# A float32 hybrid decoder layer on one core: Strassen products in the feed-forward matmuls, with the SwiGLU output kept in DRAM

## The chip, the cores and the metric

The kernel runs on one core of one Trainium2 chip. The metric is the device time of one execution in microseconds (us), lower is better. A core has engines that run side by side, each in its own order of instructions: TensorE (PE; its weight loads are listed apart as PEld), VectorE (DVE), ScalarE (ACT), GpSimd (POOL) and SyncE (SP), which here issues the DMA transfers of the weights. An engine waits for another one through semaphores.

## The reference, cut to what matters

One decoder layer for a sequence of 256 rows and a width of 2048, all in float32: a norm, an input projection, four token-mixer branches, their gated sum, an output projection, and then the feed-forward part, which is what the change touches (`w_ffn_gate` and `w_ffn_up` are 2048x5632, `w_ffn_down` is 5632x2048).

```python
        h = h + mixed @ w_out[l]
        v = rms_norm(h, norm_ffn[l])
        h = h + (jax.nn.silu(v @ w_ffn_gate[l]) * (v @ w_ffn_up[l])) @ w_ffn_down[l]
    return rms_norm(h, norm_final)
```

## The kernel before, in words

**Numbers in two parts.** A float32 factor is split into a high part (float32r, `whi`, `vth`, `hth`) and the rest (`wlo`, `vtl`, `htl`). A product of two such factors is three matmuls: high times high, high times low, low times high (`mm3`, L123 to L127). One matmul takes a 128x128 block of the activations, held transposed, as its weights and 512 columns of a weight matrix as the moving tile, and adds into a PSUM bank of 128x512.

**Weights.** `wpiece` (L112 to L121) loads 256 rows x 512 columns (512 KB, `raw`, five buffers) with a DMA issued by SP. ACT makes the high part of it (`whi`) and DVE the low part (`wlo`), each in one instruction of 128x1024. These 256 rows are called a K pair here: two blocks of 128 of the dimension summed over.

**A chunk.** `chunk` (L134 to L153) computes 512 output columns for both halves of the 256 rows, into two accumulators `acc`; of those there are four banks by turns, so that a chunk can begin while the last one is read. After the second K pair of a chunk it runs what waits in the list `later`, which is the transposing (`to_T`, L163) of the result before, on PE, ACT and DVE.

**Order of the work around the change.** Phase 3 (L645 to L671) has four chunks with `w_out`; from their result `hn` come `vth` and `vtl`, 16 blocks of K. Phase 4 (L673 to L686) has 11 steps `f`; each is one chunk with the gate matrix, SiLU on ACT, one chunk with the up matrix, and a product on DVE (`hd`); its transposed parts `hth` and `htl` stay on the core. Phase 5 (L688 on) has four chunks with `w_ffn_down` over 44 blocks of K, adds them to `hn`, and norms and stores the result. A tile framework lays each engine's instructions in order and puts a wait on a buffer where it is used again; the memory of a closed pool is given to later pools (`mx.close()`, L666, frees `mth` and `mtl`, the activations of phase 3), and then the first use of the new tile waits for the last use of the old one.

## Time and profile before

| | before |
|---|---|
| device time of three runs | 1540.54, 1544.31, 1544.32 us, median 1544.31 |
| profiled execution: span from first to last instruction | 1539.9 us |
| PE busy in the span | 1525.9 us (99%) |
| weight loads of PE | 1261.3 us (82%) |
| DVE busy | 837.8 us (54%) |
| ACT busy | 706.7 us (46%) |
| DMA | 292.11 MB, mean 190 GB/s |

The profiled execution is shown by its span; a time of its own beside it is not given. The span lies 0.6 us below the fastest of the three runs and 4.4 us below their median. Busy shares say how much of the span an engine worked, and not what it was waited for.

### The profile page before, as it was taken

To read this page: it belongs to the slowest core of one execution; us is meant where nothing else is said; L and a number is where in the kernel's file an instruction comes from. 1 tells how busy PE (TensorE), PEld (TensorE's weight loads), DVE (VectorE), ACT (ScalarE), POOL (GpSimd) and SP (SyncE) were. 2 spreads that over 40 slices of the span, in tenths; PEclk is the share of its full clock that TensorE was granted. 3 is DMA by queue.
4 is the path that set the end of the run, shared out by engine and by line. 5 is a ranking of instruction groups with operands and counts; after the bars stand their busy time and mean duration, and the time that the engine had idled before them with its cause. 6 is when DMAs were issued, how large, how long until landed. Compare 5 with 4: busy or idle time off the path is not lost.

```text
span 1539.9 us, 18236 instructions
## 1 busy us (share of the span) xinstructions
PE 1525.9 (99%) x6949; PEld 1261.3 (82%) x6949; DVE 837.8 (54%) x963; ACT 706.7 (46%) x864; POOL 94.8 (6%) x97
## 2 busy tenths in 40 slices
PE   9999999999999999999999999999999999999997
PEld 7878888888888888888888888888888888888886
DVE  5756645775565555555555455544445555444453
ACT  6545744544444444444544444444444444344342
POOL 3000300011111021010000000000000000000000
PEclk9999999999999999999999999999999999999999
DMA  8755555566666676767566666666666666666663
GB/s 256 221 150 152 158 170 152 174 182 204 200 203 198 199 206 197 205 194 243 179 182 189 190 189 188 192 186 195 188 188 191 191 190 215 193 191 193 193 193 107
DMA packets 150247, 292.11 MB, mean 190 GB/s; under 512 B 9552, under 2 KB 11664, under 8 KB 150032
## 3 DMA queue, kind: packets, MB, share of 16 engines
q1 hardware_dynamic: 148160, 285.28, 61.6%
q0 software_dynamic: 1968, 5.67, 1.4%
q8 instruction: 54, 0.88, 0.2%
q14 instruction: 33, 0.27, 0.0%
q10 hardware_dynamic: 32, 0.01, 0.0%
HBM read 288.82 MB, written 2.10 MB: 189 GB/s over the span
## 4 chain that ended last, share of the span: by engine, by line
PE 98%; DVE 1%; issue 0%; DMA 0%; POOL 0%; ACT 0%; SPq 0%; POOLq 0%; ACTq 0%
PE acc L127 94%; PE ps L159 2%; DMA xq<-in_x_dram 0%; PE ps L382 0%; PE ps L578 0%; PE ps L401 0%; PE ps L340 0%; DVE wlo L59 0%; PE ps L448 0%; PE ps L595 0%; PE ps L534 0%; PE ps L520 0%; PE ps L518 0%; POOL rq_y L59 0%; POOLq L745 0%
## 5 line engine op out<-in xcount | busy, mean ns | idle before, releaser
L59 DVE TENSOR_TENSOR wlo<-raw,whi 128x1024 fp32r<-128x1024 f32 (+1 forms) x536 | 665.6, 1242 | 654.2 <-ACT whi L56 653.2
L56 ACT ACTIVATE whi<-raw 128x1024 fp32r<-128x1024 f32 (+1 forms) x536 | 564.7, 1054 | 752.5 <-PE acc L127 709.7
L127 PE MATMUL acc<-wlo,uth 128*128 128x512 f32 (+1 forms) x832 | 323.6, 390 | 0.0
L127 PE MATMUL acc<-whi,utl 128*128 128x512 f32 (+1 forms) x832 | 323.1, 389 | 0.0
L127 PE MATMUL acc<-whi,uth 128*128 128x512 f32 (+1 forms) x832 | 317.8, 390 | 0.6 <-DVE nat L63 0.4
L127 PE MATMUL acc<-whi,vth 128*128 128x512 f32 x704 | 274.9, 390 | 0.0
L127 PE MATMUL acc<-whi,vtl 128*128 128x512 f32 x704 | 274.0, 389 | 0.0
L127 PE MATMUL acc<-wlo,vth 128*128 128x512 f32 x704 | 273.9, 389 | 0.0
L127 PEld LDWEIGHTS acc<-wlo,uth 128*128 128x128 f32 x832 | 156.9, 189 | 31.7 <-issue 1.0
L127 PEld LDWEIGHTS acc<-whi,utl 128*128 128x128 f32 x832 | 156.9, 189 | 31.4 <-issue 0.7
L127 PEld LDWEIGHTS acc<-whi,uth 128*128 128x128 f32 x832 | 154.2, 188 | 31.7 <-issue 0.7
L127 PEld LDWEIGHTS acc<-whi,vtl 128*128 128x128 f32 x704 | 132.2, 188 | 27.5
L127 PEld LDWEIGHTS acc<-whi,vth 128*128 128x128 f32 x704 | 132.2, 188 | 27.1
L127 PEld LDWEIGHTS acc<-wlo,vth 128*128 128x128 f32 x704 | 132.2, 188 | 27.0
L127 PE MATMUL acc<-whi,hth 128*128 128x512 f32 x352 | 137.0, 389 | 0.0
L127 PE MATMUL acc<-whi,htl 128*128 128x512 f32 x352 | 136.9, 389 | 0.0
L127 PE MATMUL acc<-wlo,hth 128*128 128x512 f32 x352 | 136.9, 389 | 0.0
L127 PEld LDWEIGHTS acc<-wlo,hth 128*128 128x128 f32 x352 | 66.1, 188 | 13.8
L127 PEld LDWEIGHTS acc<-whi,hth 128*128 128x128 f32 x352 | 66.1, 188 | 13.7
L127 PEld LDWEIGHTS acc<-whi,htl 128*128 128x128 f32 x352 | 66.1, 188 | 13.6
L127 PE MATMUL acc<-whi,mth 128*128 128x512 f32 x128 | 50.8, 397 | 0.0
L127 PE MATMUL acc<-wlo,mth 128*128 128x512 f32 x128 | 50.5, 395 | 0.0
...
## 6 DMA issues: line engine op xcount, KB each, us to landing
raw<-in_w_in_dram SPq DMA_DIRECT2D x192, 512.0 KB, 4.2
raw<-in_w_ffn_gate_dram SPq DMA_DIRECT2D x88, 512.0 KB, 4.4
raw<-in_w_ffn_up_dram SPq DMA_DIRECT2D x88, 512.0 KB, 3.8
raw<-in_w_ffn_down_dram SPq DMA_DIRECT2D x88, 512.0 KB, 4.8
raw<-in_w_branch_dram SPq DMA_DIRECT2D x32, 512.0 KB, 4.2
raw<-in_w_out_dram SPq DMA_DIRECT2D x32, 512.0 KB, 4.7
...
bb<-in_b_gate_dram POOLq DMA_DIRECT2D x16, 256.0 KB, 4.4
```

The costliest lines, as they stand in the source:

```text
L56: return nc.scalar.activation(o, i, f, **kw)
L59: return (eng or nc.vector).tensor_tensor(out=o, in0=a, in1=b, op=op)
L127: m = nc.tensor.matmul(acc, x_, w_, start=st, stop=sp_)
L159: nc.tensor.transpose(pt[:, i * S + t * P:i * S + (t + 1) * P], nat[:, t, (c0 + i) * P:(c0 + i + 1) * P], ident)
```

## The change

**Strassen pairs.** Of two gate and up (or two down) columns blocks of 512, and of a K pair, the old kernel makes eight block products (two row halves, two K blocks, two column blocks). Now some K pairs are made in seven products, in Winograd's form of Strassen's method: `s_weights` loads both weight blocks (`sx`, two DMAs of 512 KB), makes sums of them on DVE (`se`, and in place in `sx`), splits the four tiles in `sx` into `sh` and `sl` (128x2048) and the three in `se` into `seh` and `sel` (128x1536). The sums on the activation side are made by `s_sums` and kept in `vsh` and `vsl`. In each gate/up step the pairs are `FS` = 0, 3 and 5 of eight (0 and 3 in the first step), in each half of the down projection `DS` = 0, 3, 6, 9 and 12 of 22.

**`pair` in place of `chunk`.** It does two column blocks at once, in all eight PSUM banks, each in one buffer (`p1` to `p8`). Four hold the result of the plain products (`p2`, `p3`, `p4`, `p8`), four the Strassen products that have to be combined (`p1`, `p5`, `p6`, `p7`). After the last Strassen pair `mid` combines these on ACT and DVE (`mid_sums`, tiles `u`), and then runs the list `later`; the transposing uses the banks of `p1`, `p5`, `p6` and `p7`.

**SwiGLU output through DRAM.** `hid_out` transposes `hd` and writes it as float32 to DRAM by a DMA on POOL's queue. The down projection reads it back per K pair (`hv`, 256 KB, on SP) in each of its two halves, splits it anew into `ah`, and makes the sums for its Strassen pairs. `hv` lies in the tags `u1` and `u3` by turns, which are also the tags of two tiles of `mid_sums`; each has one buffer.

**Others.** `raw` has four buffers in place of five; the scratch pool `fp` has one buffer for each tag in place of two; all sums of the four blocks of `mid` go to `hn` in the down projection.

```diff
-        raw = wp.tile([P, nk, n], F32, tag="raw", name="raw", bufs=5)
+        raw = wp.tile([P, nk, n], F32, tag="raw", name="raw", bufs=4)
...
+                if also is not None and (kt0 + i) // 2 in also[0]:
+                    s_i = also[0].index((kt0 + i) // 2)
+                    v = late["tmp"].tile([P, 512], F32, tag="u1", name="sv").rearrange("p (a b) -> p a b", a=2)
+                    for j in range(2):
+                        act(v[:, j, :], pt[:, j * S:(j + 1) * S], scale=gcol(i + j))
+                    s_sums(v, also[1][:, s_i], also[2][:, s_i])
...
+    def s_sums(v, sh, sl):
+        w = late["tmp"].tile([P, 512], F32, tag="u0", name="ssum").rearrange("p (a b) -> p a b", a=4)
+        a11, a21, a12, a22 = v[:, 0, 0:P], v[:, 0, P:S], v[:, 1, 0:P], v[:, 1, P:S]
+        tt(w[:, 0, :], a21, a22, ALU.subtract)
+        tt(w[:, 1, :], w[:, 0, :], a11, ALU.subtract)
+        tt(w[:, 2, :], a11, a21, ALU.subtract)
+        tt(w[:, 3, :], a12, w[:, 1, :], ALU.add)
+        act(sh, w)
+        tt(sl, w, rd(sh), ALU.subtract)
+    def mm3s(acc, a, w, first, last, pin=False):
+        for x_, w_, st, sp_ in ((a[0], w[0], first, False), (a[0], w[1], False, False), (a[1], w[0], False, last)):
+            m = nc.tensor.matmul(acc, x_, w_, start=st, stop=sp_)
+            if pin:
+                tc.keep_in_program_order(m)
...
+    def s_weights(wl, wr, kp, sx):
+        rows = slice(kp * 2 * P, (kp + 1) * 2 * P)
+        x_ = sx.tile([P, 4, 512], F32, tag="sx", name="sx", bufs=2)
+        nc.sync.dma_start(x_[:, 0:2, :], wr[rows, :].rearrange("(k p) n -> p k n", p=P))
+        nc.sync.dma_start(x_[:, 2:4, :], wl[rows, :].rearrange("(k p) n -> p k n", p=P))
+        e = sx.tile([P, 3, 512], F32, tag="se", name="se", bufs=1)
+        h, lo = (sx.tile([P, 4, 512], F32R, tag=t, name=t, bufs=2) for t in ("sh", "sl"))
+        eh, el = (sx.tile([P, 3, 512], F32R, tag=t, name=t, bufs=2) for t in ("seh", "sel"))
+        tt(e[:, 0, :], x_[:, 0, :], x_[:, 1, :], ALU.add)
+        tt(x_[:, 0, :], x_[:, 0, :], x_[:, 2, :], ALU.add)
+        tt(e[:, 1, :], x_[:, 0, :], x_[:, 1, :], ALU.add)
+        tt(e[:, 2, :], e[:, 1, :], x_[:, 3, :], ALU.add)
+        act(h, x_)
+        tt(lo, x_, rd(h), ALU.subtract)
+        act(eh, e)
+        tt(el, e, rd(eh), ALU.subtract)
+        t1, r2, l1, l2 = ((h[:, i, :], lo[:, i, :]) for i in range(4))
+        t3, t2, t4 = ((eh[:, i, :], el[:, i, :]) for i in range(3))
+        return l1, l2, r2, t1, t2, t3, t4
+    def pair(wl, wr, nkp, skps, a_of, sx, mid, split=0):
+        pq = late["psum"]
+        names = (1, 5, 7, 6, 2, 3, 4, 8) if skps else (2, 3, 4, 8)
+        b = {i: pq.tile([P, 512], F32, tag=f"p{i}", name=f"p{i}") for i in names}
+        left = {2: nkp * 2 - len(skps), 3: nkp * 2 - len(skps), 4: nkp * 2 - len(skps), 8: 2 * (nkp - len(skps))}
+        for i in (1, 5, 6, 7):
+            left[i] = len(skps)
+        begun = set()
+        def go(i, a, w, pin=False):
+            left[i] -= 1
+            mm3s(b[i], a, w, i not in begun, left[i] == 0, pin)
+            begun.add(i)
+        held = []
+        for kp in range(nkp):
+            blk, sums = a_of(kp, kp in skps)
+            if kp in skps:
+                l1, l2, r2, t1, t2, t3, t4 = s_weights(wl, wr, kp, sx)
+                go(1, blk(0, 0), l1)
+                go(5, sums(0), t1)
+                go(7, sums(2), t3)
+                go(6, sums(1), t2)
+                go(2, blk(1, 0), l2)
+                go(3, sums(3), r2)
+                go(4, blk(1, 1), t4)
+                if kp == skps[-1]:
+                    mid(b)
+                continue
+            if not skps and kp == 2:
+                mid(b)
+            rows = slice(kp * 2 * P, (kp + 1) * 2 * P)
+            lh, ll = wpiece(wl[rows, :], 2, 512)
+            rh, rl = wpiece(wr[rows, :], 2, 512)
+            todo = [(i, [(blk(j, t), (wh[:, j, :], wl_[:, j, :])) for j in range(2)])
+                    for i, t, wh, wl_ in ((2, 0, lh, ll), (3, 0, rh, rl), (4, 1, lh, ll), (8, 1, rh, rl))]
+            if kp >= nkp - split:
+                held.append(todo)
+                continue
+            for i, prods in todo:
+                for a, w in prods:
+                    go(i, a, w)
+        for q in range(4):
+            for todo in held:
+                i, prods = todo[q]
+                for a, w in prods:
+                    go(i, a, w, pin=True)
+        return b
...
+    FS = (0, 3, 5)
+    late["tmp"] = fp
+    vsh = fp.tile([P, len(FS), 4, P], F32R, name="vsh")
+    vsl = fp.tile([P, len(FS), 4, P], F32R, name="vsl")
...
+    ps_early.close()
+    late["psum"] = ctx.enter_context(tc.tile_pool(name="pq", bufs=1, space=bass.MemoryType.PSUM))
+    sx = ctx.enter_context(tc.tile_pool(name="sxp", bufs=1))
...
+    def hid_out(hd, f):
+        hs = fp.tile([P, 4, S], F32, tag="hs", name="hs")
+        for i in (0, 2):
+            pt = trans_bank(hd, i, 2)
+            act(hs[:, i:i + 2, :].rearrange("p a b -> p (a b)"), pt)
+        d = dr.tile([P, 4, S], F32, name=f"hid{f}")
+        nc.gpsimd.dma_start(d, hs)
+        hid.append(d)
...
+    def mid_sums(b):
+        u = [fp.tile([P, 512], F32, tag=f"u{i}", name="u") for i in range(4)]
+        act(u[0], b[1])
+        tt(u[2], u[0], b[6], ALU.add)
+        tt(u[1], u[2], b[7], ALU.add)
+        tt(u[2], b[5], u[2], ALU.subtract)
+        tt(u[3], b[5], u[1], ALU.subtract)
+        return u
...
     for f in range(DFF // 512):
         fs = slice(f * 512, (f + 1) * 512)
-        ag = chunk(w_fg[:, fs], vth, vtl, NKT)
+        kept = []
+        def mid(b):
+            kept.extend(mid_sums(b))
+            run_later()
...
         hd = fp.tile([P, 2, 512], F32, tag="hd", name="hd")
         for t in range(2):
-            act(hd[:, t, :], ag[t], AF.Silu, scale=rstd2[:, t:t + 1])
-        au = chunk(w_fu[:, fs], vth, vtl, NKT)
-        for t in range(2):
-            stt(hd[:, t, :], au[t], rstd2[:, t:t + 1], hd[:, t, :], ALU.mult, ALU.mult)
-        later.append(lambda hd=hd, f=f: to_T(hd, hth, htl, 4 * f))
-    # ================= phase 5: down projection, final norm =================
+            tt(hd[:, t, :], kept[t], b[(2, 4)[t]], ALU.add)
+            act(hd[:, t, :], hd[:, t, :], AF.Silu, scale=rstd2[:, t:t + 1])
+            tt(kept[2 + t], kept[2 + t], b[(3, 8)[t]], ALU.add)
+            stt(hd[:, t, :], kept[2 + t], rstd2[:, t:t + 1], hd[:, t, :], ALU.mult, ALU.mult)
+        later.append(lambda hd=hd, f=f: hid_out(hd, f))
...
+    ah = uv.tile([P, 4, 2, 2 * S], F32R, tag="tl", name="ah")
+    DS = (0, 3, 6, 9, 12)
+    def h_of(kp, with_sums):
+        v = fp.tile([P, 512], F32, tag=("u1", "u3")[kp % 2], name="hv").rearrange("p (a b) -> p a b", a=2)
+        nc.sync.dma_start(v, hid[kp // 2][:, kp % 2 * 2:kp % 2 * 2 + 2, :])
+        q = kp % 4
+        act(ah[:, q, 0, :], v.rearrange("p a b -> p (a b)"))
+        tt(ah[:, q, 1, :], v.rearrange("p a b -> p (a b)"), rd(ah[:, q, 0, :]), ALU.subtract)
+        if with_sums:
+            i = DS.index(kp) % len(FS)
+            s_sums(v, hsh[:, i], hsl[:, i])
+        def blk(j, t):
+            o = slice(j * S + t * P, j * S + (t + 1) * P)
+            return ah[:, q, 0, o], ah[:, q, 1, o]
+        return blk, lambda n: (hsh[:, i, n, :], hsl[:, i, n, :])
...
+    for cc in range(2):
+        cols = [slice((2 * cc + i) * 512, (2 * cc + i + 1) * 512) for i in range(2)]
+        def mid(b):
+            u = mid_sums(b)
+            for t in range(2):
+                for i in range(2):
+                    o = hn[:, t, cols[i]]
+                    tt(o, o, u[2 * i + t], ALU.add)
+            run_later()
+        b = pair(w_fd[:, cols[0]], w_fd[:, cols[1]], NFT // 2, DS, h_of, sx, mid, split=2 if cc else 1)
```

In the excerpts that follow, each row is an instruction: line, operation, out<-in, size, and in brackets the engine or DMA queue whose semaphore it waits for. Line numbers are those of the kernel that the row is from. A name ends in a number that tells one buffer's use from another.

**First place: SP, from the last weights of the output projection on, before.**

```order
L114 DMA raw_6353<-in_w_out_dram 128x2x512 [waits DMAHW6_49,DVE_49]
L114 DMA raw_6371<-in_w_out_dram 128x2x512 [waits DMAHW7_49,DVE_49]
L114 DMA raw_6416<-in_w_ffn_gate_dram 128x2x512 [waits DMAHW0_49,DVE_49]
L114 DMA raw_6434<-in_w_ffn_gate_dram 128x2x512 [waits DMAHW1_49,DVE_49]
L114 DMA raw_6470<-in_w_ffn_gate_dram 128x2x512 [waits DMAHW2_49,DVE_49]
```

The same place on SP after the change.

```order
L120 DMA raw_6538<-in_w_ffn_up_dram 128x2x512 [waits DMAHW4_49,DVE_49]
L120 DMA raw_6632<-in_w_ffn_gate_dram 128x2x512 [waits DMAHW5_49,DVE_49]
L120 DMA raw_6638<-in_w_ffn_up_dram 128x2x512 [waits DMAHW6_49,DVE_49]
L120 DMA raw_6668<-in_w_ffn_gate_dram 128x2x512 [waits DMAHW7_49,DVE_49]
L220 DMA sx_6459<-in_w_ffn_up_dram 128x2x512 [waits DMASW3_49,DMASW4_49,DMASW2_49,DMASW5_49,DMASW1_49,DMASW6_49,DMASW0_49,DMASW7_49,PE_49,Pool_49]
L221 DMA sx_6459<-in_w_ffn_gate_dram 128x2x512
L220 DMA sx_6568<-in_w_ffn_up_dram 128x2x512
L221 DMA sx_6568<-in_w_ffn_gate_dram 128x2x512
L120 DMA raw_6674<-in_w_ffn_up_dram 128x2x512 [waits DMAHW0_49,DVE_49]
```

Behind the last load of `w_out` stand seven `raw` loads now, the last four of which are shown (K pairs 2 and 4, and the gate half of 5), and only then the loads of `sx_6459`, for K pair 0; the first of the two waits for PE and POOL: the pool of `sx` takes memory of `mth` and `mtl`, and its first tile waits for the last matmul that reads them.

**Second place: DVE, from the last gate/up step to the down projection, before** (`acc_9691` and `acc_9692` are that step's up chunk, `raw_9895` is a tile of `w_ffn_down`).

```order
L59 TENSOR_TENSOR wlo_9898<-raw_9895,whi_9897 128x1024 [waits DMAHW7_49,Activation_49]
L67 SCALAR_TENSOR_TENSOR hd_9688<-acc_9691,rstd2_6397,hd_9688 128x512 [waits PE_49]
L67 SCALAR_TENSOR_TENSOR hd_9688<-acc_9692,rstd2_6397,hd_9688 128x512 [waits PE_49]
L59 TENSOR_TENSOR wlo_9916<-raw_9913,whi_9915 128x1024 [waits DMAHW0_49,Activation_49]
L59 TENSOR_TENSOR wlo_9934<-raw_9931,whi_9933 128x1024 [waits DMAHW1_49,Activation_49]
```

The same place on DVE after the change (`hv_10118` is K pair 0 of the down projection, `hv_10166` K pair 1).

```order
L60 TENSOR_TENSOR hd_10096<-u_10001,p4_9779 128x512 [waits PE_49]
L60 TENSOR_TENSOR se_10388<-sx_10385 128x512 [waits DVE_49]
L60 TENSOR_TENSOR wlo_10213<-raw_10210,whi_10212 128x1024 [waits DMAHW5_49,Activation_49]
L60 TENSOR_TENSOR u_10003<-u_10003,p8_9780 128x512 [waits PE_49]
L68 SCALAR_TENSOR_TENSOR hd_10096<-u_10002,rstd2_6429,hd_10096 128x512 [waits DVE_49,Activation_49]
L60 TENSOR_TENSOR se_10388<-se_10388,sx_10385 128x512 [waits DVE_49]
L60 TENSOR_TENSOR wlo_10219<-raw_10216,whi_10218 128x1024 [waits DMAHW6_49,Activation_49]
L68 SCALAR_TENSOR_TENSOR hd_10096<-u_10003,rstd2_6429,hd_10096 128x512 [waits DVE_49,Activation_49]
L60 TENSOR_TENSOR ssum_10122<-hv_10118 128x128 [waits DMAHW3_49]
L60 TENSOR_TENSOR ssum_10122<-hv_10118 128x128
L60 TENSOR_TENSOR ssum_10122<-ssum_10122,hv_10118 128x128 [waits DVE_49]
L60 TENSOR_TENSOR ah_10109<-hv_10118,ah_10109 128x512 [waits Activation_49]
```

And SP there, after the change (before, only loads of `raw` stood there).

```order
L120 DMA raw_10298<-in_w_ffn_down_dram 128x2x512 [waits DMAHW1_49,DVE_49]
L120 DMA raw_10304<-in_w_ffn_down_dram 128x2x512 [waits DMAHW2_49,DVE_49]
L852 DMA hv_10118<-hid0_7034 128x512 [waits DMAHW3_49,DMASW1_49,DVE_49]
L120 DMA raw_10338<-in_w_ffn_down_dram 128x2x512 [waits DMAHW5_49,DMAHW4_49,DVE_49]
L120 DMA raw_10344<-in_w_ffn_down_dram 128x2x512 [waits DMAHW6_49,DVE_49]
L852 DMA hv_10166<-hid0_7034 128x512 [waits DVE_49]
L852 DMA hv_10206<-hid1_7366 128x512 [waits DMAHW3_49,DMASW2_49,DMAHW7_49,DVE_49,Activation_49]
L852 DMA hv_10246<-hid1_7366 128x512 [waits DMAHW6_49,DMAHW0_49,DVE_49]
```

The step's own results are now joined from six sums with `u` tiles and two products, with sums and splits for K pairs of the down projection between them. The load of `hv_10118` uses the tag `u1` and stands behind the reading of `u_10001`; that of `hv_10166` uses `u3` and stands behind the reading of `u_10003` (`hd_10096<-u_10003`).

**Third place: DVE in the down projection, where accumulators are read, before** (the end of the first chunk).

```order
L59 TENSOR_TENSOR wlo_10304<-raw_10301,whi_10303 128x1024 [waits DMAHW5_49,Activation_49]
L59 TENSOR_TENSOR hn_5708<-hn_5708,acc_9843 128x512 [waits PE_49]
L59 TENSOR_TENSOR hn_5708<-hn_5708,acc_9844 128x512 [waits PE_49]
L59 TENSOR_TENSOR wlo_10322<-raw_10319,whi_10321 128x1024 [waits DMAHW6_49,Activation_49]
L59 TENSOR_TENSOR wlo_10340<-raw_10337,whi_10339 128x1024 [waits DMAHW7_49,DVE_49,Activation_49]
```

DVE in the middle of the first half of the down projection, behind its last Strassen pair (K pair 12), after the change.

```order
L60 TENSOR_TENSOR hn_5708<-hn_5708,u_10678 128x512 [waits Activation_49]
L60 TENSOR_TENSOR u_10680<-u_10678,p6_10113 128x512 [waits PE_49]
L60 TENSOR_TENSOR u_10679<-u_10680,p7_10112 128x512 [waits DVE_49]
L60 TENSOR_TENSOR u_10680<-p5_10111,u_10680 128x512 [waits DVE_49]
L60 TENSOR_TENSOR u_10681<-p5_10111,u_10679 128x512
L60 TENSOR_TENSOR hn_5708<-hn_5708,u_10679 128x512
L60 TENSOR_TENSOR hn_5708<-hn_5708,u_10680 128x512 [waits DVE_49]
L60 TENSOR_TENSOR sl_11234<-sx_11229,sh_11233 128x2048 [waits Activation_49]
L60 TENSOR_TENSOR hn_5708<-hn_5708,u_10681 128x512 [waits DVE_49]
L60 TENSOR_TENSOR sel_11236<-se_11232,seh_11235 128x1536 [waits Activation_49]
L60 TENSOR_TENSOR ah_10109<-hv_10746,ah_10109 128x512 [waits DMAHW2_49,Activation_49]
```

And SP there, after the change.

```order
L120 DMA raw_10830<-in_w_ffn_down_dram 128x2x512 [waits DMAHW2_49,DVE_49]
L120 DMA raw_10836<-in_w_ffn_down_dram 128x2x512 [waits DMAHW3_49,DVE_49]
L852 DMA hv_10746<-hid7_9358 128x512 [waits DMASW0_49,DVE_49]
L220 DMA sx_11485<-in_w_ffn_down_dram 128x2x512 [waits DVE_49]
L221 DMA sx_11485<-in_w_ffn_down_dram 128x2x512 [waits DMAHW4_49]
L852 DMA hv_10706<-hid6_9026 128x512 [waits DMAHW5_49,DVE_49]
L852 DMA hv_10826<-hid8_9690 128x512 [waits DMAHW2_49,DMAHW6_49,DMASW1_49,DVE_49]
L852 DMA hv_10786<-hid7_9358 128x512 [waits DMAHW7_49,DMAHW5_49,DVE_49]
```

Before, two sums clear the banks, and no load waits for them. Now `hv_10746` (K pair 14) uses `u1` and waits for the sum that reads `u_10679`; `hv_10706` (K pair 13) uses `u3`, stands behind both loads of `sx_11485`, and waits for the sum that reads `u_10681`. On PE the last Strassen pair is followed by nine matmuls of it and eight transposes, and then by K pair 13.

## Rows read from the trace of the kernel before

**Rows 1.** The page: span, engines, granted clock, chain by engine.
```profile
span 1539.9 us, 18236 instructions
...
PE 1525.9 (99%) x6949; PEld 1261.3 (82%) x6949; DVE 837.8 (54%) x963; ACT 706.7 (46%) x864; POOL 94.8 (6%) x97
...
PEclk9999999999999999999999999999999999999999
...
PE 98%; DVE 1%; issue 0%; DMA 0%; POOL 0%; ACT 0%; SPq 0%; POOLq 0%; ACTq 0%
```
**Rows 2.** Chain that ended last, gate/up steps and down: start, us, work.
```profile
807.31 43.54 PE acc L127 x192
851.72 43.55 PE acc L127 x192
...
1251.51 43.54 PE acc L127 x192
1295.92 228.52 PE acc L127 x1008
```
**Rows 3.** Busy time by stretch: a gate/up step, then part of the down projection.
```profile
core 0: us, PE busy (x) PEld busy (x) DVE busy (x) ACT busy (x) POOL busy (x), PEclk, DMA share, GB/s
851.70:896.10 44.40, 44.40 (x202) 36.85 (x201) 22.13 (x20) 19.18 (x21) 0.00 (x0) 1.00 0.65 190
1355.80:1415.00 59.20, 59.20 (x262) 49.02 (x262) 28.29 (x25) 24.68 (x26) 2.96 (x2) 1.00 0.62 192
```
**Rows 4.** Groups, 851.7 to 1296 us: busy us, mean ns, idle before, releaser.
```profile
L59 DVE TENSOR_TENSOR wlo<-raw,whi 128x1024 fp32r<-128x1024 f32 x160 | 196.1, 1226 | 222.9 <-ACT whi L56 222.9
L56 ACT ACTIVATE whi<-raw 128x1024 fp32r<-128x1024 f32 x161 | 170.7, 1060 | 244.0 <-PE acc L127 244.0
...
L67 DVE SCALAR_TENSOR_TENSOR hd<-acc,rstd,hd 128x512 f32<-128x512 f32 x20 | 14.0, 743 | 0.0
...
L59 DVE TENSOR_TENSOR htl<-ps,hth 128x512 fp32r<-128x512 f32 x20 | 12.8, 683 | 0.0
L56 ACT ACTIVATE hth<-ps 128x512 fp32r<-128x512 f32 x20 | 10.7, 585 | 0.0
L159 PE MATMUL ps<-ident,hd 128*128 128x128 f32 x81 | 10.6, 272 | 0.0
```
**Rows 5.** Groups of the whole run, the other shapes.
```profile
L56 ACT ACTIVATE whi<-raw 128x772 fp32r<-128x772 f32 x16 | 13.5, 846 | 6.0 <-DMA raw<-in_w_in_dram 5.9
...
L67 DVE SCALAR_TENSOR_TENSOR L<-nbd,ps 128x128 f32<-128x128 f32 x8 | 1.9, 284 | 2.7 <-PE ps L382 2.7
...
L59 DVE TENSOR_TENSOR hn<-hn,gfin 128x512 f32<-128x512 f32 x2 | 1.4, 688 | 0.0
```
**Rows 6.** DMA issues: transfer, count, size of each, median us from issue to landing.
```profile
raw<-in_w_ffn_gate_dram SPq DMA_DIRECT2D x88, 512.0 KB, 4.4
raw<-in_w_ffn_up_dram SPq DMA_DIRECT2D x88, 512.0 KB, 3.8
...
bb<-in_b_gate_dram POOLq DMA_DIRECT2D x16, 256.0 KB, 4.4
...
out_dram<-hn SPq DMA_DIRECT2D x8, 256.0 KB, 3.0
```
**Rows 7.** The `raw` tiles: SP's time for an issue in ns, and landing.
```profile
L114 SPq DMA_DIRECT2D raw<-in_w_ffn_gate_dram x88: 367/368/368, 780.1 to 1244.9; - x88
...
DMA to landing us min/median/max: 3.0/4.4/10.4
```
**Rows 8.** Busy time by stretch at the start; columns as in rows 3.
```profile
6.00:8.00 2.00, 0.09 (x1) 0.12 (x2) 1.85 (x3) 1.22 (x3) 0.64 (x2) 1.00 0.97 129
8.00:10.00 2.00, 2.00 (x11) 1.81 (x12) 0.86 (x2) 1.24 (x4) 0.59 (x1) 0.63 1.02 383
10.00:12.00 2.00, 2.00 (x7) 1.61 (x7) 1.27 (x2) 1.91 (x5) 1.68 (x3) 0.51 1.05 394
```
**Rows 9.** PE's waits in the whole run: us, times, longest.
```profile
PE ps L159 <- DMA xq<-in_x_dram: 2.0, 1, 2.0
PE ps L198 <- DVE zb L193: 1.3, 1, 1.3
```
**Rows 10.** Timeline: last matmul of the output projection, first of gate/up.
```profile
800.56 0.40 PE L127 MATMUL acc<-whi,mtl 128*128 128x512 f32 x1
800.79 0.40 PE L127 MATMUL acc<-whi,vth 128*128 128x512 f32 x1
```

More of the change, by code (lines that the diff above doesn't have):

```diff
@@ L67, in stt @@
         return nc.vector.scalar_tensor_tensor(out=o, in0=a, scalar=s, in1=b, op0=op0, op1=op1, **kw)
+    late = {"psum": None, "turn": 0}
     def bank():
[L70 removed]
+        if late["psum"] is None:
+            return psb.tile([P, 512], F32, tag="ps", name="ps")
+        late["turn"] = (late["turn"] + 1) % 4
+        return late["psum"].tile([P, 512], F32, tag=f"p{(1, 5, 7, 6)[late['turn']]}", name="ps")
     def rd(t):
@@ new lines, in v_of, with sums @@
+    def v_of(kp, with_sums):
+        def blk(j, t):
+            o = slice(t * P, (t + 1) * P)
+            return vth[:, 2 * kp + j, o], vtl[:, 2 * kp + j, o]
+        def sums(i):
+            q = FS.index(kp)
+            return vsh[:, q, i, :], vsl[:, q, i, :]
+        return blk, sums
+    def mid_sums(b):
[6 more added lines that the diff above has]
+        return u
@@ L692, in hybrid_block_kernel @@
     pre3 = small.tile([P, 2], F32, name="pre3", bufs=1)
-    for c in range(4):
-        cs = slice(c * 512, (c + 1) * 512)
-        acc = chunk(w_fd[:, cs], hth, htl, NFT, tail=8 if c == 3 else 0)
-        for t in range(2):
-            tt(hn[:, t, cs], hn[:, t, cs], acc[t], ALU.add)
-            sumsq(ss3[:, t, c:c + 1], hn[:, t, cs])
-            if c < 3:
-                tt(hn[:, t, cs], hn[:, t, cs], gfin[:, cs], ALU.mult, nc.gpsimd)
+    ah = uv.tile([P, 4, 2, 2 * S], F32R, tag="tl", name="ah")
@@ L701, in hybrid_block_kernel @@
                 continue
-            ms3, r, z, r3 = (small.tile([P, 1], F32, tag=f"r3{i}", name="r3") for i in range(4))
-            stt(ms3, ss3[:, t, 3:4], 1.0 / D, pre3[:, t:t + 1], ALU.mult, ALU.add)
+            ms3, r, z, r3, p3 = (small.tile([P, 1], F32, tag=f"r3{i}", name="r3") for i in range(5))
+            nc.vector.tensor_reduce(out=p3, in_=ss3[:, t, 0:3], axis=AX.X, op=ALU.add)
+            ts(p3, p3, 1.0 / D, EPS, ALU.mult, ALU.add)
+            stt(ms3, ss3[:, t, 3:4], 1.0 / D, p3, ALU.mult, ALU.add)
```

37 lines of the change are left out of this document (23 added, 14 removed).

## The prediction

> **What bounds the kernel now.** I began with the page [rows 1]: PE is busy for 99% of the span, its granted clock is full in every slice, and the chain that ended last is PE for 98%. Next the chain by stages [rows 2]: a gate/up step is 192 matmuls in 43.54 us, so one 128x512 matmul costs 43.54/192 = 0.2268 us, and steps follow at 44.42 us (851.72 less 807.31, and the like), of which eight transposes take 44.42 - 43.54 = 0.88. The down projection is one run of 1008 matmuls that the chain does not leave. The stretches say how much room the others have [rows 3]: in a gate/up step DVE works 22.13 of 44.40 us, ACT 19.18, DMA 0.65 of its time; in the down projection DVE 28.29 of 59.20. Before a group of DVE or ACT, the idle time ends with ACT, and ACT's with PE [rows 4]: both wait for PE, not the other way. PE itself waited for 2.0 and 1.3 us at the two longest places of the whole run [rows 9], and it goes over from the output projection to gate/up with no gap: 800.79 follows 800.56 by 0.23 us [rows 10]. So each matmul taken away is worth its 0.2268 us as long as nothing else makes PE wait, and each new wait of PE is paid in full.
>
> **The matmuls removed.** A Strassen pair has 7x3 = 21 matmuls in place of 8x3 = 24. There are 2 + 10x3 = 32 of them in gate/up and 2x5 = 10 in the down projection: 42x3 = 126 matmuls fewer, -126 x 0.2268 = **-28.6 us**. The transposes stay as many.
>
> **What DVE and ACT get.** A plain K pair costs DVE 2x1.226 = 2.45 us [rows 4]. A Strassen pair costs four sums of 128x512 (0.683 to 0.688 each, [rows 4, 5]), a split of 128x2048 and one of 128x1536. Neither size is in the trace; from 512 columns at 0.688 to 1024 at 1.226 the price grows by 0.538 for 512, which gives 1.76 and 2.30: 2.75 + 4.06 = 6.8 us. If DVE went at the first 512 columns' rate instead, they would cost 2.06 and 2.75, 7.6 in all. Added up by the DVE order of one gate/up step (five plain pairs, three Strassen pairs, ten sums with `u` and two products of 0.743), DVE works 39.6 us a step, and PE 183 x 0.2268 + 0.88 = 42.4. Thus DVE is busy for 93%, but PE is still the longer of the two; I put 1 us on small waits there (0 to 8). At the higher price it would be 42.0, just level. ACT's splits of 2048 and 1536 columns, by its 846 ns for 772 and 1060 for 1024 [rows 4, 5], are 1.93 and 1.50 against 2.12 for a plain pair; ACT stays far below PE.
>
> **Place 1, into gate/up.** The loads of `sx_6459` wait for the last matmul of the output projection. Two issues take 0.37 each [rows 7]; the second half lands 3.0 (the minimum) to 4.4 us (the median) after its issue [rows 6, 7], behind `raw` loads still under way. Then one or two sums of 0.69, ACT's `sh` 1.93. So the first Strassen matmul comes 0.74 + 3.0 to 4.4 + 0.69 + 1.93 = 6.4 to 7.8 us after that matmul, and `sl` (2.30) and `seh` (1.50) hold it up by 1 to 2 more behind the few matmuls on `sh` alone. PE has 12 `p8` matmuls to do, 2.7 us: a stall of 5 to 7. The first step also meets `vth` 12 to 15 late, since their transposing stands behind its `mid`, some 1.5. Together **+8** (5 to 10).
>
> **Place 2, into the down projection.** Let the last gate/up matmul end at T. The load of `hv_10118` waits for DVE's sum with `u_10001`, about T + 1.5 (two or three sums of 0.68, some of it before T). Issue 0.37, landing 3.0 (256 KB stored by SP took that, 256 KB on POOL's queue 4.4, [rows 6]), ACT 0.6 ([rows 4], `hth`): PE begins at T + 5.5 to 7. `hv_10166`, for K pair 1, waits for the last product, which DVE reaches after two sums with `u` and `sx`, two `wlo` and two products, T + 7.4; and so its matmuls begin at 7.4 + 0.37 + 3.3 + 0.6 + 0.7 = T + 12.4. K pair 0 is 21 x 0.2268 = 4.8 us of work, so K pair 1 comes **7.6** us late (6 to 9.5).
>
> **Place 3, the middle of the first down half.** Let the last `p6` matmul end at B. PE has nine matmuls and eight transposes left, 2.9 us, and then needs K pair 13. The load of `hv_10706` stands behind both loads of `sx_11485` and behind DVE's `hn` sum with `u_10681`: by the third excerpt that is seven sums of 0.68 and one split of 2.30, 7.1 us after B at the soonest. With 0.37, 3.0 and 0.6 PE goes on at B + 11.1: a stall of 8. DVE is not on time there. K pair 3 uses `u3` behind K pair 1, split at T + 12.4: its load lands at 16.1, and its sums end at about T + 18. From there DVE's rows up to this place add up to 59.7 us, which is T + 78. PE, from T + 12.4 on, has eight plain pairs and four Strassen pairs less nine matmuls, 267 x 0.2268 = 60.6, and is there at T + 73. So DVE is 5 us late, and 1 MB of `sx` lands ahead of `hv`. I take **+13** (8 to 16).
>
> **Place 4, the same in the second half**, with no Strassen weights to come: no split of 2.30 and no `sx` ahead. **+8.5** (6 to 11).
>
> **The clock.** At the start of the run PE did nearly nothing from 6 to 8 us, and was granted 0.63 and 0.51 of its clock in the two stretches after it, at 8 to 12 us [rows 8]; it was at 1.2 GHz then for most of 4 us, and full again from 12. Four us at half rate lose 2. Each of the four places has a longer idle than that one; where the data come late anyway, the slow clock is hidden. I take **+5** of 4x2 = 8 (0 to 8). The Trainium skill (TensorE: Matmul & The Clock Gate, section HAM oscillation — how this bites in real kernels) describes the same: waits for DMA between bursts of matmuls let the clock fall, and it reports a slowed time of 1.67 us for each, half of which is lost. By that figure the four places would cost 4 x 0.83 = 3.3 us, an estimate; the trace here shows a slowed stretch about twice as long.
>
> **What costs nothing.** The 11 writes of `hid` go on POOL's queue, which has nothing else to do; the reads are 2 x 22 x 256 KB = 11 MB in 220 us, on a DMA at 0.62 to 0.65 [rows 3], and what hides them is PE's work on the K pairs ahead, two buffers of `hv` deep; without that cover they are what places 2 to 4 already count. For four `raw` buffers in place of five I add **+1** (0 to 3): SP's issues come as far ahead as buffers allow, and the landing median is 4.4 us against two K pairs of PE, 10.9. The end of the run has the same chain as before.
>
> **Sum.** -28.6 + 8 + 7.6 + 13 + 8.5 + 5 + 1 + 1 = **+15.5 us**. On the span of 1539.9 that is 1555; the runs lie up to 4.4 above the span, and their median of 1544.3 gives **1560 us**. With all low ends it is -28.6 + 5 + 6 + 8 + 6 = -3.6, 1541; with the high ones -28.6 + 10 + 9.5 + 16 + 11 + 8 + 3 + 8 = +37, 1581.
>
> **Rivals.** A change of under 0.3%, 4.6 us, can't be told from none here.
>
> *The `hv` loads do not hold PE up* (the other side). If SP can issue them early, because DVE is ahead and clears `u1` and `u3` while PE still works, places 2 to 4 and their clock go: 15.5 - 29.1 - 3.8 = -17.4, 1527. For it: DVE and SP always wait for PE now [rows 4], and loads are early in all of this run [rows 9]. Against it: the sums at the end of a block need PE's last products, so that no tag can be free before these; PE's cover behind them is 2.9 us, and the landing alone takes 3.0. It decides if the three places cost less than 9 us and not 29. Chance 0.2.
>
> *The stalls are near their low ends*: -3.6 up to +4, 1541 to 1548, nothing that can be measured. It needs landings of 3.0 us, a DVE that is on time at place 3 and no loss of clock. Chance 0.13.
>
> *DVE becomes the bound of gate/up.* If the long splits or the sums in PSUM cost 10% more, a step on DVE takes 43.6 and not 39.6, PE's 42.4 are passed, and ten steps give +12; with the added waits on single `u` and `se` buffers, up to +20: 1572 to 1580. For it: 93% by the order's rows. Against it: 1.226 us was steady over 160 splits [rows 4]. Chance 0.12.
>
> The forecast itself, stalls above the saving and gate/up bound by PE, 1549 to 1572: 0.55.
>
> **How the numbers follow.** Faster: the first rival, 0.2. Same: the second, 0.13. Slower: 0.55 + 0.12 = 0.67. The range must leave out no more than 2 in 10, from both ends: down to 1536 it takes in the low ends and leaves out most of the first rival, up to 1576 half of the third; **1536 to 1576**. The forecast's own range is 1549 to 1572.
>
> **What would show it.** PE's waits: four new ones of 5 to 15 us in front of `sh_6463`, of the first and second K pair of the down projection, and behind the last Strassen pair of each half, put down to DMA or to ACT and DVE behind it; the granted clock low in the stretches after them; gate/up steps at 42.4 us with DVE at 93%. The saving is right if matmuls in gate/up still start every 0.227 us. The forecast is wrong if places 2 to 4 show waits of under 3 us each, or if steps follow at more than 43 us.

## The result and the profile after

The changed kernel takes 1554.98 us (median of four runs, 1553.21 to 1560.77) against 1544.08 for the kernel before (1540.54 to 1544.32; a fourth run, of 1543.85, has come to the three of the table). The ratio is 1.0085, with a 95% interval from 1.0063 to 1.0106: it is slower by 10.9 us. The forecast was 1560, slower, with a range of 1536 to 1576.

The page of the changed kernel has these rows for [rows 1]. PE is busy for 19.6 us less than before, and the span is 12.4 us longer. The chain that ended last has lost 8% to DVE, DMA and issue.

```profile
span 1552.3 us, 18562 instructions
...
PE 1506.3 (97%) x6823; PEld 1243.3 (80%) x6823; DVE 1088.4 (70%) x1324; ACT 794.3 (51%) x940; POOL 102.0 (7%) x108
...
PEclk9999999999999999999999999999999999989999
...
PE 90%; DVE 4%; DMA 3%; issue 2%; ACT 1%; SPq 0%; POOL 0%; POOLq 0%; ACTq 0%; DVEq 0%
```

PE's waits from 795 us on (releaser, us in total, times, longest), where before there was none [rows 9]:

```profile
PE p L213 <- ACT ah L57: 22.4, 3, 11.4
PE p L213 <- ACT sh L57: 5.6, 1, 5.6
PE p L213 <- DVE hn L60: 1.0, 1, 1.0
```

The three waits for `ah` are those in front of the down projection (4.87 us, to 1283.80) and behind the last Strassen pair of its two halves (11.43, to 1365.30, and 6.13, to 1489.92); the wait for `sh` ends at 811.58. Busy time by stretch shows each wait and then the 6 us after it; the first row is two gate/up steps, as [rows 3] has one of before. Columns: stretch, length, busy us and instructions of PE, PEld, DVE, ACT, POOL, granted clock, DMA share, GB/s.

```profile
1058.98:1143.86 84.88, 84.88 (x384) 70.28 (x383) 73.95 (x77) 46.38 (x42) 1.07 (x2) 1.00 0.66 211
805.80:811.60 5.80, 0.18 (x2) 0.02 (x1) 3.27 (x9) 1.99 (x2) 0.00 (x0) 0.83 1.00 371
811.60:817.60 6.00, 6.00 (x17) 4.72 (x18) 5.90 (x5) 1.90 (x2) 0.00 (x0) 0.60 0.43 134
1278.80:1283.80 5.00, 0.13 (x1) 0.00 (x0) 5.00 (x8) 2.72 (x4) 0.54 (x1) 1.00 1.02 383
1283.80:1289.80 6.00, 6.00 (x19) 4.82 (x20) 2.29 (x8) 1.42 (x3) 0.00 (x0) 0.72 0.76 267
1352.80:1365.30 12.50, 1.07 (x10) 0.80 (x8) 10.68 (x14) 5.12 (x7) 0.53 (x1) 0.75 0.73 246
1365.30:1371.30 6.00, 6.00 (x18) 4.78 (x19) 1.99 (x3) 1.20 (x2) 0.00 (x0) 0.66 0.31 97
1483.60:1489.90 6.30, 0.19 (x1) 0.00 (x0) 3.53 (x6) 1.26 (x2) 0.00 (x0) 0.92 0.46 154
1489.90:1495.90 6.00, 5.98 (x14) 4.68 (x15) 2.08 (x3) 1.26 (x2) 0.00 (x0) 0.52 0.43 131
```

A step takes 84.88/2 = 42.44 us where it took 44.42 [rows 2]: the saving is there in full, PE is busy all the time, and DVE has 87%. In the 6 us behind each wait PE is busy throughout, but the granted clock is 0.60, 0.72, 0.66 and 0.52: 6 x (0.40 + 0.28 + 0.34 + 0.48) = 9.0 us are lost (the clock is granted at one of two levels, 1.2 and 2.4 GHz; a share between 0.5 and 1 is a mean over the 6 us). The account of the span: -28.6 for the matmuls, +29.0 for the three rows of waits, +9.0 for the clock, +1.05 because the output projection ended later (its last matmul starts at 801.61, before at 800.56 [rows 10]); that is +10.5 of the +12.4, and the other 2 are small gaps and the end. The 1.05 hides two things that were not forecast: the start of the run was 3.45 us slower, and what follows up to the end of the output projection 2.4 us faster; the last section has both.

### The profile page after: what moved, and what is told of

It reads as the page before. It is cut to its first block, busy times and chain, and to the rows that moved or that the text cites. A ratio compares the mean times of both kernels' runs of the same rounds, so it can differ in the third digit from the quotient of the medians.

```text
span 1552.3 us, 18562 instructions
## 1 busy us (share of the span) xinstructions
PE 1506.3 (97%) x6823; PEld 1243.3 (80%) x6823; DVE 1088.4 (70%) x1324; ACT 794.3 (51%) x940; POOL 102.0 (7%) x108
## 4 chain that ended last, share of the span: by engine, by line
PE 90%; DVE 4%; DMA 3%; issue 2%; ACT 1%; SPq 0%; POOL 0%; POOLq 0%; ACTq 0%; DVEq 0%
PE acc L133 47%; PE p L213 38%; DMA hv<-hid 2%; PE ps L165 2%; DVE wlo L60 1%; DVE sl L60 1%; DVE se L60 1%; DVE u L60 1%; DMA xq<-in_x_dram 0%; DMA sx<-in_w_ffn_gate_dram 0%; DVE hn L60 0%; PE ps L489 0%; PE ps L685 0%; PE ps L508 0%; PE ps L447 0%
## 5 line engine op out<-in xcount | busy, mean ns | idle before, releaser
L60 DVE TENSOR_TENSOR wlo<-raw,whi 128x1024 fp32r<-128x1024 f32 (+1 forms) x452 | 560.9, 1242 | 336.6 <-ACT whi L57 332.7
L57 ACT ACTIVATE whi<-raw 128x1024 fp32r<-128x1024 f32 (+1 forms) x452 | 474.8, 1052 | 526.4 <-PE acc L133 304.5
L213 PE MATMUL p<-whi,ah 128*128 128x512 f32 x544 | 172.2, 396 | 17.6 <-ACT ah L57 17.6
L213 PE MATMUL p<-whi,vth 128*128 128x512 f32 x448 | 175.2, 391 | 1.0 <-DVE hn L60 1.0
L213 PE MATMUL p<-wlo,vth 128*128 128x512 f32 x448 | 175.1, 391 | 0.0
L213 PE MATMUL p<-whi,vtl 128*128 128x512 f32 x448 | 174.3, 391 | 0.0
L213 PEld LDWEIGHTS p<-whi,ah 128*128 128x128 f32 x544 | 104.2, 191 | 40.1 <-ACT ah L57 18.2
L60 DVE TENSOR_TENSOR sl<-sx,sh 128x2048 fp32r<-128x2048 f32 x42 | 96.1, 2288 | 50.1 <-ACT sh L57 50.1
L213 PE MATMUL p<-wlo,ah 128*128 128x512 f32 x272 | 107.8, 397 | 0.0
L213 PEld LDWEIGHTS p<-whi,vth 128*128 128x128 f32 x448 | 84.2, 188 | 18.5 <-issue 1.4
```

The lines of the kernel that those rows point to most:

```text
L57: return nc.scalar.activation(o, i, f, **kw)
L60: return (eng or nc.vector).tensor_tensor(out=o, in0=a, in1=b, op=op)
L213: m = nc.tensor.matmul(acc, x_, w_, start=st, stop=sp_)
```

## The experiments

All times are medians beside runs of the kernel before on the same chip, which took 1542.95 to 1543.81 us there; 1544.08 beside the changed kernel. So differences between one experiment and another are good to about 1 us.

### The way back from DRAM: the raw ring in place of the tags of the sums

```diff
-        v = fp.tile([P, 512], F32, tag=("u1", "u3")[kp % 2], name="hv").rearrange("p (a b) -> p a b", a=2)
-        nc.sync.dma_start(v, hid[kp // 2][:, kp % 2 * 2:kp % 2 * 2 + 2, :])
+        if kp % 2 == 0:
+            four[0] = wp.tile([P, 4, S], F32, tag="raw", name="hv", bufs=4)
+            nc.sync.dma_start(four[0], hid[kp // 2])
+        v = four[0][:, kp % 2 * 2:kp % 2 * 2 + 2, :]
```

> The changed kernel, but the SwiGLU output is read back through the ring of raw weight buffers (one load of 512 KB for two K pairs) and no longer through the tags u1 and u3. Theory of the waits: PE's 11.4 and 6.1 us waits behind the last Strassen pair of each down half and the slow clock behind them go, the 4.9 us wait into the down projection shrinks to 1 to 3; 1555 becomes 1533 to 1540. Rival, VectorE itself is too slow in the down projection: it stays late by about 5 us in each half, and the time stays at 1547 or more. Rival, the pass through DRAM costs by its traffic: no change, 1553 to 1557.

Measured: 1531.53 us, ratio 0.9926 (0.9911 to 0.9941), 23.5 less than the changed kernel and faster than before; it is 1.5 below the range of the theory of the waits, on the side away from both rivals. PE's longest waits in it:

```profile
PE p L213 <- ACT sh L57: 5.8, 1, 5.8
PE ps L165 <- DMA xq<-in_x_dram: 2.1, 1, 2.1
PE ps L165 <- ACT dqn L57: 1.4, 1, 1.4
PE p L213 <- ACT ah L57: 1.4, 1, 1.4
```

The waits for `ah` have gone from 22.4 to 1.4 us; only place 1, untouched, is left. DVE does the same sums and splits, and the same bytes go through DRAM, so neither rival holds: it was a load that waits for a buffer which the last sums free. The edit takes that wait away in two ways at once, which were not told apart: `hv` no longer shares a tag with the `u` tiles, and one load brings two K pairs, so that K pair 13 comes with K pair 12. Of the first down half those two are issued at 1330.34 and K pairs 14 and 15 at 1335.04, and the sums behind the last Strassen pair begin at 1350.8.

### The first Strassen weights: three plain K pairs ahead

```diff
-        b = pair(w_fg[:, fs], w_fu[:, fs], NKT // 2, FS[:2] if f == 0 else FS, v_of, sx, mid, split=1)
+        b = pair(w_fg[:, fs], w_fu[:, fs], NKT // 2, FS[1:2] if f == 0 else FS, v_of, sx, mid, split=1)
```

> The changed kernel, but the first gate/up step has one Strassen pair, K pair 3, in place of 0 and 3, so that three plain K pairs (16 us of PE) lie ahead of the first Strassen weights. Theory of the waits: the 5.6 us wait on sh and the slow clock after it go, three matmuls (0.7 us) come back: 1545 to 1549. Rival, another wait takes its place, because the transposed tiles 12 to 15 and VectorE are just as late: 1552 or more.

Measured: 1548.09 us, ratio 1.0033 (1.0021 to 1.0046), 6.9 less than the changed kernel. The wait for `sh` is not in its trace any more, and no other has come in its place; the waits for `ah` are much as they were (23.3 us, longest 12.1). The wait of 1.0 us for `hn` is still there, as it is with no Strassen pair at all, so it does not belong to place 1.

### Both repairs

The two edits above together.

> Both repairs: the SwiGLU output read back through the raw ring, and K pair 3 as the only Strassen pair of the first gate/up step. The two gains were 23.5 and 6.9 us apart; if the places are independent they add up: 1523 to 1526. Rival, with PE never waiting VectorE is the next bound and takes part of it back: 1528 or more.

Measured: 1524.78 us, ratio 0.9872 (0.9855 to 0.9888): 30.2 us less than the changed kernel, where the two gains were 23.5 and 6.9. The gains add up, as the expectation had it, and at 1.3% below the kernel before the seven products do pay.

They pay in gate/up alone. These are the lengths of the two stages, gate/up and then the down projection, in the kernel before and then with both repairs (from 0.23 us after the start of the last matmul of the stage ahead, to the same place at the stage's end, or to the end of the last matmul; columns as above):

```profile
800.79:1289.44 488.65, 488.65 (x2202) 405.64 (x2200) 244.64 (x229) 214.41 (x227) 0.72 (x1) 1.00 0.64 189
1289.44:1529.87 240.43, 240.43 (x1065) 198.91 (x1063) 116.31 (x105) 97.24 (x103) 10.43 (x8) 1.00 0.58 183
```
```profile
804.43:1274.14 469.71, 468.73 (x2108) 387.38 (x2107) 413.35 (x434) 260.51 (x240) 6.08 (x11) 1.00 0.66 216
1274.14:1514.96 240.82, 236.08 (x1035) 192.73 (x1034) 190.72 (x242) 130.88 (x157) 11.30 (x9) 1.00 0.66 219
```

Gate/up is 18.9 us shorter, with 93 matmuls fewer (21.1 us). The down projection has 30 matmuls fewer, 6.8 us, and is as long as before: PE is idle for 4.7 us of it, in small waits for DVE and ACT (`wlo` 1.7 in three, `ah` 1.6 and 1.2), and some matmuls follow each other more slowly. So ten of the Strassen pairs gain next to nothing even with both repairs. What is behind those small waits was not tried, nor a plain down projection with the raw ring.

### No Strassen pair, the rest as changed

```diff
-    DS = (0, 3, 6, 9, 12)
+    DS = ()
...
-            kept.extend(mid_sums(b))
...
-        b = pair(w_fg[:, fs], w_fu[:, fs], NKT // 2, FS[:2] if f == 0 else FS, v_of, sx, mid, split=1)
+        b = pair(w_fg[:, fs], w_fu[:, fs], NKT // 2, (), v_of, sx, mid, split=1)
```

SiLU and the product then read the accumulators, as in the kernel before, and `mid` only runs the list.

> No Strassen pair anywhere, all else as in the changed kernel: two column blocks at once, single PSUM banks, the SwiGLU output through DRAM, four raw buffers. Theory of the waits: the 28.6 us come back, the waits before sh and behind the last Strassen pairs are gone, the one into the down projection stays in part: 1545 to 1551, just above the kernel before. Rival, the pass through DRAM and the new order cost much by themselves: 1556 or more, so that the Strassen products would have been a gain.

Measured: 1544.78 us, ratio 1.0015 (1.0005 to 1.0026), 0.2 below the low end of what the theory of the waits gave. No wait for `ah` stands among its PE rows: without `u` tiles the tags of `hv` are free early. So the pass through DRAM, the two column blocks at once and the single banks cost 1 to 2 us together on the whole run. In the trace their two stages are 490.38 and 241.34 us long, 2.6 more than before, and the output projection is 2.4 us shorter, for a reason that is open (last section); that hides most of it. The Strassen pairs with both repairs, 123 matmuls fewer, save 1544.78 - 1524.78 = 20.0 of 27.9 us.

### Strassen in one of the two stages

The changed kernel with plain products in the down projection (`DS = ()`, no sums in its `mid`), and with plain products in gate/up (`FS` not used).

> The changed kernel with no Strassen pair in the down projection (30 matmuls, 6.8 us, come back there); gate/up and the pass through DRAM as changed. Theory of the waits: the two waits behind the last Strassen pairs and their clock, 22.7 us, go; place 1 (10 us) and most of place 2 (6 us) stay; 1555 + 6.8 - 22.7 is 1539, 1536 to 1542. Rival, the single buffer for the SwiGLU output's tags holds the down projection up by itself: 1548 or more.

> The changed kernel with no Strassen pair in gate/up (96 matmuls, 21.8 us, come back); the down projection as changed. Theory of the waits: place 1 (10 us) goes, places 2 to 4 (29 us) stay: 1555 + 21.8 - 10 is 1567, 1563 to 1570. Rival, VectorE's load of the gate/up steps is what makes it late in the down projection, so that the waits there shrink with it: 1558 or less.

Measured: 1537.73 us, ratio 0.9962 (0.9950 to 0.9974), and 1562.44, ratio 1.0121 (1.0106 to 1.0136). The first is in its range: gate/up alone, even with place 1 unrepaired, is a gain. The second is 0.6 us below its range. PE's waits say why:

```profile
PE p L213 <- ACT ah L57: 18.4, 3, 11.5
```

Of these three the ones behind the last Strassen pairs are 11.5 and 6.2 us, as before; the one left near place 2 is only 0.7, and it comes at 1303.32, 10 us into the down projection. Plain gate/up steps have no `u` tiles, so `u1` and `u3` were free early. The expectation had left place 2 its 6 us, though its own theory takes them away: 1555 + 21.8 - 10 - 6 is 1561.

### Four raw buffers in the kernel before

```diff
-        raw = wp.tile([P, nk, n], F32, tag="raw", name="raw", bufs=5)
+        raw = wp.tile([P, nk, n], F32, tag="raw", name="raw", bufs=4)
```

> The kernel before with four raw buffers in place of five. Prediction's term: 0 to 3 us more, 1544 to 1547. The rival puts more on it: the start of the run loses 3 us as in the changed kernel, and the matmuls of the output projection go back from 0.2333 to 0.2267 us each, 2.5 us less, because the buffers lie elsewhere in memory; then the total is near 1544 to 1545 with both to be seen in the trace.

Measured: 1545.59 us, ratio 1.0015 (1.0006 to 1.0025), some 2 us more, within the prediction's 0 to 3. The rival's first half is seen in this one profile, where the last long run of the input projection begins at 609.47, as in the changed kernel; but the version with no Strassen pair has four buffers too and begins at 606.54, so the buffers are not shown to be its cause. The rival's second half falls: in the output projection this kernel has the same chain row as the kernel before, and the changed kernel has another. First a row of the chain before, then of this one, then of the changed kernel (start, us, work), all three of the second chunk of the output projection.

```profile
737.61 22.40 PE acc L127 x96
```
```profile
741.04 22.40 PE acc L127 x96
```
```profile
740.33 21.82 PE acc L133 x96
```

### More Strassen pairs, and the loads on another queue

Seven Strassen pairs in each down half, on top of both repairs:

```diff
-    DS = (0, 3, 6, 9, 12)
+    DS = (0, 3, 6, 9, 12, 15, 18)
```

> As e6_both, with seven Strassen pairs (0, 3, ..., 18) in place of five in each half of the down projection: 12 matmuls, 2.7 us, fewer. PE stays the bound: 1520 to 1523. VectorE is the bound: its 4 x 4.4 us more are paid in part, and the time is that of e6_both or above, 1525 to 1533.

Measured: 1531.86 us, ratio 0.9915 (0.9898 to 0.9932), 7 us above both repairs alone. (The profiled execution is the fastest of the four, 1526.92; it had a start 4 us quicker than the profile of both repairs. Its down projection is 245.83 us long, 5.0 more.) But nothing there looks like a DVE that is short of time: PE has one single new wait, in the first half, and no other of more than 2 us.

```profile
PE p L213 <- ACT whi L57: 9.9, 1, 9.9
```

I took it for SyncE's order, since a load of `sx` had held that queue before it (its row: `sx` waiting for DVE's `sl`, 13.7 us), and moved these loads:

```diff
-        nc.sync.dma_start(x_[:, 0:2, :], wr[rows, :].rearrange("(k p) n -> p k n", p=P))
-        nc.sync.dma_start(x_[:, 2:4, :], wl[rows, :].rearrange("(k p) n -> p k n", p=P))
+        nc.gpsimd.dma_start(x_[:, 0:2, :], wr[rows, :].rearrange("(k p) n -> p k n", p=P))
+        nc.gpsimd.dma_start(x_[:, 2:4, :], wl[rows, :].rearrange("(k p) n -> p k n", p=P))
```

> e8_seven with the Strassen weight loads (sx) on POOL's queue and no longer on SyncE's. In e8 SyncE stood from 1363 to 1377 us at a load of sx that waited for VectorE's split of the pair before, and PE then waited 9.9 us for plain weights queued behind it. Theory of the queue: that wait goes, and the 12 matmuls fewer show: 1519 to 1524, at or below e6_both's 1525. Rival, VectorE has no room for two more pairs a half: 1528 or more, as e8.

Measured: 1535.61 us, ratio 0.9952 (0.9935 to 0.9969): the theory that this load alone was the cause fell. PE's wait of 9.7 us is still there, and the longest wait of SyncE's queue from 1360 to 1400 us names another releaser:

```profile
SPq L854 <- DMA hid<-hs: 23.8, 1, 23.8
```

In this version SyncE is at the read of the last piece of the SwiGLU output, and waits for its write, which POOL issues at 1384.63. (With `sx` on SyncE's queue the write was issued at 1375.32, while SyncE still stood at `sx`, and the read at 1378.41 had no wait for it: two waits that follow the same sums lay one behind the other.) That piece can be transposed only when `mid` has freed the banks, behind the last Strassen pair; at K pair 18 of 22 that is too close to K pair 20, which needs it, and plain weights stand in the queue behind that read. The second half has no such write, so seven pairs there alone should go, with the `sx` loads on SyncE's queue again:

```diff
-        b = pair(w_fd[:, cols[0]], w_fd[:, cols[1]], NFT // 2, DS, h_of, sx, mid, split=2 if cc else 1)
+        b = pair(w_fd[:, cols[0]], w_fd[:, cols[1]], NFT // 2, DS if cc else DS[:5], h_of, sx, mid, split=2 if cc else 1)
```

> e8_seven, but with seven Strassen pairs in the second down half only, five in the first, six matmuls (1.4 us) fewer than e6_both. In e8 and e9 SyncE waited at the read of the last piece of the SwiGLU output for its write, which can be made only after the last Strassen pair of the first half has freed the banks for its transposes, and plain weights queued behind that read. Theory of that wait: it goes, as the second half has no such write: 1521 to 1525. Rival, VectorE has no room for more pairs: 1528 or more, with PE's wait now in the second half.

Measured: 1521.56 us, ratio 0.9865 (0.9848 to 0.9881), in the range of the third theory, and PE has no wait for `whi` of more than 0.2 us. It is the lowest median of all, but its interval overlaps that of both repairs; the trace has a down projection of 238.89 us, 1.9 less than there, for six matmuls (1.4 us) fewer. A stretch of its second down half, with DVE at 87% and PE without a gap:

```profile
1400.00:1500.00 100.00, 100.00 (x441) 82.34 (x441) 87.15 (x107) 55.51 (x62) 2.97 (x2) 1.00 0.64 210
```

The same move of the `sx` loads was made in the changed kernel, and in the one with both repairs:

> The changed kernel with the sx loads on POOL's queue. In the first down half the read of the SwiGLU output then no longer stands behind two loads of sx on SyncE, but still waits for the sum that frees its tag: that wait of 11.4 us becomes 8 to 9.5, the others stay: 1550 to 1554. Rival, the order on SyncE is all of that wait: it falls below 5 us, and the time to 1548 or less. Loads from POOL's queue may also cost more and land later: 1557 or more.

> e6_both with the sx loads on POOL's queue. PE hardly waits there now, so there is little to gain: 1522 to 1526. If POOL's queue is dearer, 1528 or more.

Measured: 1549.45 us, ratio 1.0049 (1.0030 to 1.0067), and 1527.03, ratio 0.9900 (0.9886 to 0.9915). The first time is 0.6 below its range. In this run PE's wait at place 3 is 5.4 us in place of 11.4, further down than expected, but not below the rival's 5. Two things moved at once: the two loads of `sx` are out of the way of `hv`, and DVE does its three sums into `hn` ahead of the split `sl` now, so the tag is free 2.3 us sooner. What each of the two is worth was not told apart. Place 2 grew from 4.9 to 8.4 us, and in the second run from 1.6 to 3.8; why was not looked into. The second is 2.2 us above the version without the move, between its two expectations; POOL's queue gains nothing when SyncE's has no such wait.

## Why the prediction was right

**The saving.** 126 matmuls at 0.2268 us: the step row of 42.44 us shows it. Right.

**Place 1** (+8, and 1 to 2 for its clock). PE waited 5.6 us for `sh` and lost 2.4 at the slow clock: 8.0, where 9 to 10 were forecast. Taking the place away gave 6.9, with three matmuls, 0.7 us, put back. The wait of 1.0 for `hn` was not in the sum and is no part of this place.

**Place 2** (+7.6). The mechanism was right, and the sum came near by luck, since two sizes were off against each other. The last gate/up matmul starts at 1278.55, so T is 1278.78. The two loads were issued sooner than forecast, at T - 0.3 and T + 5.1 in place of T + 1.5 and T + 7.4, and landed later, 4.6 and 5.1 us after the issue in place of 3.0 and 3.3:

```profile
1278.48 0.34 SPq L852 DMA_DIRECT2D hv<-hid  x1
1283.12 0.63 ACT L57 ACTIVATE ah<-hv 128x512 fp32r<-128x512 f32 x1 [2.23 <-DMA hv<-hid]
1283.88 0.69 SPq L852 DMA_DIRECT2D hv<-hid  x1
1289.00 1.28 ACT L57 ACTIVATE ah<-hv 128x512 fp32r<-128x512 f32 x2 [3.07 <-DMA hv<-hid]
```

The 3.0 was read from `out_dram<-hn` [rows 6], a store; the 44 loads of `hv` here take 2.5 to 7.1 us to land, median 4.2. PE began 5.0 us after T, near the 5.5 forecast, and did K pair 0 half at the slow clock; K pair 1 began at 1290.27, T + 11.5 and not T + 12.4. So it came 6.7 us late, and no wait is to be seen in front of it, since the slow clock filled the time.

**Place 3** (+13, and its clock). Measured 11.4 and 2.0. The sum is near by luck: two terms are off, one each way. DVE was to be 5 us late, and was 1: the last `p6` matmul ended at 1350.8 and the sums that read it began at 1351.81. The load of `hv` was to land in 3.0 us, and it took 5.6 behind 1 MB of `sx`: issued at 1358.98, its split on ACT starts at 1364.61. (The prediction named the `sx` ahead and gave it no price.)

```profile
1350.57 0.39 PE L213 MATMUL p<-seh,vsl 128*128 128x512 f32 x1
1351.81 1.41 DVE L60 TENSOR_TENSOR u<-u,p 128x512 f32<-128x512 f32 x2
1357.86 0.69 DVE L60 TENSOR_TENSOR hn<-hn,u 128x512 f32<-128x512 f32 x1
1358.98 7.96 SPq L852 DMA_DIRECT2D hv<-hid  x4
1364.61 1.25 ACT L57 ACTIVATE ah<-hv 128x512 fp32r<-128x512 f32 x2 [6.17 <-DMA hv<-hid]
```

The 5 us of DVE went wrong because I added durations of single instructions. This part of DVE's timeline in the changed kernel has starts 0.60 us apart for durations of 0.68:

```profile
1276.58 0.68 DVE L60 TENSOR_TENSOR sx<-sx 128x512 f32<-128x512 f32 x1
1277.18 0.68 DVE L60 TENSOR_TENSOR u<-u,p 128x512 f32<-128x512 f32 x1
1277.78 0.68 DVE L60 TENSOR_TENSOR hd<-u,p 128x512 f32<-128x512 f32 x1
1278.37 0.69 DVE L60 TENSOR_TENSOR se<-sx 128x512 f32<-128x512 f32 x1
```

Most instructions that follow each other overlap by 0.08 us, as here; the four sums of `sx` and `se` at 1360.73, 1361.45, 1362.17 and 1362.90, which hang on one another, do not and start 0.72 apart for 0.69. From 1296.8 to 1351.8 DVE has 66 instructions, 61 of which overlap with the one ahead: that is the 5 us. The trace of before could have told it: in this row of its timeline two sums of 0.68 take 1.28 together.

```profile
800.43 1.28 DVE L59 TENSOR_TENSOR hn<-hn,acc 128x512 f32<-128x512 f32 x2
```

**Place 4** (+8.5, and its clock). 6.1 and 2.9. With no `sx` loads ahead the last of the chain's loads of `hv` landed in 2.75 us, near the 3.0.

**DVE in gate/up** (93% forecast, PE still the bound). 73.95 of 84.88 us is 87%: the same overlap, on 38 instructions a step. (The forecast's 39.6 comes out with eight sums with `u`, which the kernel has, and not with the ten of its text, which would give 41.0.) The two sizes that the trace did not have came out as extrapolated, 2.30 and 1.76 (mean ns in the row, then idle before and its releaser):

```profile
L60 DVE TENSOR_TENSOR sl<-sx,sh 128x2048 fp32r<-128x2048 f32 x42 | 96.1, 2288 | 50.1 <-ACT sh L57 50.1
...
L60 DVE TENSOR_TENSOR sel<-se,seh 128x1536 fp32r<-128x1536 f32 x42 | 73.6, 1752 | 1.1 <-ACT seh L57 1.1
```

So the rival that makes DVE the bound of gate/up is out, and the two with seven pairs that ran slow were slow for another reason.

**The clock** (+5 of at most 8). 9.0 were lost at four places, 2.25 each, in 6 us at a granted clock between 0.52 and 0.72. The term was too small: it hid 3 of its 8 us behind late data, and PE was busy in all these 6 us. Some was hidden even so, at place 2: at 0.2268 each the 21 matmuls of K pair 0 would have ended at 1288.56, and the first split for K pair 1 was done at 1289.63, so that of the 1.7 us lost there about 1.1 would have been a wait at the full clock (an estimate). The Trainium skill (TensorE: Matmul & The Clock Gate, section HAM oscillation — how this bites in real kernels) reports 1.67 us at half rate behind each wait, which by its figure would be 0.83 us lost at a place, an estimate. Here it was more than twice that, and the measurement decides.

**The rest.** Four raw buffers: 0.9 to 3.9 us by the interval of that run, 1 in the sum. From the start of the last matmul to the end of the span it takes 10.9 us, before 10.4.

The sum of the four places and the clock was 42.1 and measured 38.0 (29.0 + 9.0, with the 1.0 for `hn`). With the saving it would have given +13.5 and +9.4. So the account holds by place and by cause; that the single sums came this near is in part luck, in the two places above and in the start and the output projection, which moved the run by +3.45 and -2.4 us and are in no term. The rival on the other side, in which `hv` does not hold PE up, is the kernel with the raw ring: it was forecast at 1527 and measured 1531.5, with place 1 still in it.
